# The tokens of the last two expert places, not of the last alone, get ends of their own in a decoder layer with experts

## The chip, the cores and the metric

One core of a Trainium2 chip runs the whole layer as one program. The metric is the device time of one execution in microseconds, the median of several. The kernel before takes 2732.44 us, the median of 3 runs (2731.12 to 2740.7).

## What is computed

One decoder layer over 4096 tokens of width 1024: attention heads and gated recurrent heads side by side, a residual, and then a mixture of experts. Only its last part matters here:

```
h = rmsnorm(x, ln2_pre) * (1 + sc2) + sh2
g_w, g_idx = top_k(softmax(h @ w_rg + b_rg), 1)          # 1 of 4 groups
e_w, e_idx = top_k(softmax(e_logits[of that group]), 2)  # 2 of its 8 experts
ys  = (silu(h @ w_gate[e]) * (h @ w_up[e])) @ w_down[e]  # for both experts
y   = sum over both of ys * weight
out = x + ga2 * rmsnorm(y, ln2_post)
```

Each token meets two experts of one group. Its end, the norm of the sum and the addition to x, needs both results.

## The kernel before, in words

**Sweeps.** `sweep1` and `sweep2` compute the first part. `sweep2` writes x to `out`, the normed tokens to `h_d`, and routes batches of tokens (`g_route`, line 1469): for each of a token's two choices a row of three words (token, row of its result, weight) is scattered to the table `tab_d`, at a slot of its expert, and the token's number to the list `list_d`, in the order of its group. `g_const` (line 1181) fills both tables beforehand. Experts are then ordered by load into 32 places: 8 places for each group, each with a fixed capacity (`CAPS`, line 1717; places 28 to 31 have 256 rows, two tiles of 128).

**Between.** `order` (line 1720) gathers the table by places, transposes its three columns on TensorE, and gets `tokid`, `yrow` and `wgt` for each place, and `last`, tokens and rows of place 31.

**Experts.** `experts` (line 1842) runs the places 0 to 31 on TensorE. For each: load gate, up and down weights (1 MB each, by SP, into the ring `WS` of 4 slots), split each into a high and a low part (ScalarE and VectorE, ring `W` of 8), gather the tokens (GpSimd, ring `XG` of 4), transpose and split them (ring `XT` of 13), gate and up products (`gate_up`), activation, and down products (`down`, line 1924), whose weighted results `g_put` (line 2138) scatters by GpSimd to `y_d`, one row for each choice of each token, the two rows of a token next to each other.

**Ends.** The 4096 tokens of the list are 32 tiles, 8 for each group. `g_fin(m)` (line 2186) ends tile m when all places of its group have put their results: SP reads the tile's 256 rows (1 MB) into a slot of `YY` (2 slots) or, for the last group, of `WS` or `W`; VectorE adds the pairs, ScalarE squares and sums, GpSimd computes the norm's factor (`rstd`, two small operations named `rfv` and `rfr`), VectorE scales, and GpSimd adds the rows to `out` by an indirect store (`put_out`), one small store to `spacer` ahead of it. Entries of the list that lie past the end are skipped by the store.

The tokens of place 31, the last, are not ended through the list. `g_list` (line 2163) writes zeros to their rows of `y_d` and puts a number past the end in their places in the list. `g_other` (line 2213) gathers the results of their other choices from `y_d`, once all other places have put theirs. `down` for place 31 adds this to its product, and `g_last` (line 2155) norms and stores it (`rlv`, `rlr`, `out_dram<-y,last`). `list_rows` (line 1795) computes the indices for this. The last group's list tiles wait for the gathers of `g_other`:

```
rings = [YY]
if g == 3:
    while ("other", tile_n[31] - 1) not in st:
        yield WAIT
    rings += [WS, W]
```

**What sets the order.** All of this is written as generators (lines of work), which `Weave` (line 159) interleaves by a modelled clock: a line goes on when what it names (a tile, an engine) is ready by that clock. So the order on each engine is fixed when the program is built. Each engine's queue is then taken in that order, and a wait stands in front of all that was put behind it: SP's queue carries the weight loads and the reads of `y_d`, GpSimd's all indirect transfers, the small norm operations and the stores to `out`. Transfers that write the same tile, or read what another wrote, wait for the earlier one to land, except where `no_dep` (line 289) says that they don't touch the same rows.

The profile gives line 140 for nearly every instruction, because a wrapper there records them; groups are told apart by tile.

Of the kernel before, what the change touches and what calls it, by code (L numbers as in the profile page):

```python
# [21 lines left out]
P = 128  # L22
# [250 lines left out]
class Layer:  # L273
# [59 lines left out]
    def setup(self, ctx):  # L333
# [807 lines left out]
    def sweep2(self, w16a):  # L1141
# [7 lines left out]
        with ExitStack() as ctx:  # L1149
# [31 lines left out]
            def g_const():  # L1181
# [38 lines left out]
                fill = op.tile([P, D], F32, name="xr")  # L1220
                nc.gpsimd.memset(fill, float(16 * T))
# [247 lines left out]
            def g_route(m):  # L1469
# [85 lines left out]
                nc.vector.tensor_sub(gm[:, 3], gm[:, 3], gm[:, 2])  # L1555
                pl = tile([P, RB, 2, 3], F32, "pl2", 2)[:, :B]
                nc.vector.tensor_copy(pl[:, :, :, 0], bc(idi[:, n0:n0 + B], 2))
# [162 lines left out]
    def order(self, cp, rp, rps):  # L1720

        nc, T, NT = self.nc, self.T, self.NT
        cnt = self.place[:, 1]
# [27 lines left out]
        pt = rps.tile([P, 3, P], F32, name="ps_x")  # L1751
        for o in range(3):
            nc.tensor.transpose(pt[:, o], trow[:, :, o], self.ident)
# [41 lines left out]
    def list_rows(self, cp, rp):  # L1795
# [16 lines left out]
        nc.vector.tensor_scalar(out, out, 1, None, op0=ALU.logical_shift_right)  # L1812
        other = cp.tile([P, 4], I32, name="other")
        nc.vector.tensor_scalar(other, self.yrow[:, P - 4:], 1, None, op0=ALU.bitwise_xor)
        yield
        of = rp.tile([P, 2, 4], F32, name="of4")
        nc.vector.tensor_copy(of[:, 0], out)
        nc.vector.tensor_copy(of[:, 1], other)
        yield
        nc.vector.scalar_tensor_tensor(out, gid[:, 3:4].to_broadcast([P, 4]), float(T), of[:, 0],  # L1820
                                       op0=ALU.mult, op1=ALU.add)
        nc.vector.tensor_scalar_min(other, of[:, 1], float(2 * T - 1))
        self.other = other
# [18 lines left out]
    def experts(self):  # L1842
# [5 lines left out]
        with ExitStack() as ctx:  # L1848
# [74 lines left out]

            def down(avs, wd, j, m, y, wgt, other=None):
                for c in range(2):
                    yield ["ps_d"]
                    pd = ps_d.tile([P, 512], F32, name="ps_d")[:m]
                    for f in range(2):
                        yield [avs[f]]
                        for n, (u, v) in enumerate(((0, 0), (1, 0), (0, 1))):  # L1930
                            nc.tensor.matmul(pd, avs[f][:, u, j * P:j * P + m], wd[f][:, v, c * 512:(c + 1) * 512],
                                             start=(f == 0 and n == 0), stop=(f == 1 and n == 2))
                    v = slice(c * 512, c * 512 + 512)
                    if other is None:
                        self.copy(y[:m, v], pd, wgt)
                    else:
                        nc.vector.scalar_tensor_tensor(y[:m, v], pd, wgt, other[:m, v], op0=ALU.mult, op1=ALU.add)
# [49 lines left out]
            with tc.For_i(0, n_over, 1) as it:  # L1987
# [6 lines left out]
                nc.vector.tensor_scalar_min(oi[:, 1:2], oi[:, 1:2], float(32 * T - 1))  # L1994
                pf = fp.tile([P, 3], F32, name="pf")
                self.gather(pf, self.tab_d, oi[:, 1:2])
# [120 lines left out]
            def g_down(r, avs):  # L2117
# [5 lines left out]
                for j in range(tile_n[r]):  # L2123
                    m = min(P, C - j * P)
                    y = yield from Y.take()
                    wgt = self.wgt[:m, 4 * r + j:4 * r + j + 1]
                    if r < 31:
# [7 lines left out]
                    we.add(g_last(y, o, j, m), first=True)  # L2135
# [18 lines left out]

            def g_last(y, o, j, m):

                yield [y]
                yield from norm(y[:m], o[:m], "rl")
                put_out(y[:m], self.last[:m, 0, j:j + 1])

            ti = cp.tile([P, NT], I32, name="ti")

            def g_list():
# [22 lines left out]
            def g_fin(m):  # L2186
# [96 lines left out]
```

## Time and profile before

| | before |
|---|---|
| median of 3 runs | 2732.44 us |
| profiled execution: own time | 2765.53 us |
| profiled execution: span | 2763.8 us |
| TensorE busy | 2510.2 us (91%) |
| VectorE busy | 1905.7 us (69%) |
| ScalarE busy | 1360.1 us (49%) |
| GpSimd busy | 756.7 us (27%) |
| mean granted TensorE clock | 0.961 of 2.4 GHz |

The span is the time from the first to the last instruction of the profiled execution; its own time is that of the whole execution. Profiling makes it longer than the median of the plain runs. Busy time is the time in which an engine worked on some instruction. Times within the span are counted from its start.

### The profile page before, as it was taken

Reading aid. Unit: us, or ns where it says so; the run is one execution under the profiler, and the core shown is the slowest. Engines: PE = TensorE matmul, PEld = TensorE weight load, DVE = VectorE, ACT = ScalarE, POOL = GpSimd, SP = SyncE. Lnnn points to the kernel's source line nnn. Section 1 sums busy time; section 2 is a strip of 40 time slices with the busy share of each in tenths; the row PEclk is TensorE's granted clock in tenths of the full one; section 3 lists DMA queues with packets and bytes.
Section 4 is the critical chain, followed back from the end, with each engine's and each line's share of the span. In section 5 each row is a group of like instructions: output and inputs, shape, how many; then the busy total and the mean of one; then the engine's idle time right before and its main releaser. Section 6 shows DMA issues by size and latency. Waiting matters only on the chain. (4 is left out here: it accounts for less than half of the span.)

```text
span 2763.8 us, 50275 instructions
## 1 busy us (share of the span) xinstructions
PE 2510.2 (91%) x19433; PEld 1916.5 (69%) x19433; DVE 1905.7 (69%) x4109; ACT 1360.1 (49%) x2935; POOL 756.7 (27%) x1069
## 2 busy tenths in 40 slices
PE   5989999999999999989999999955999999999992
PEld 2767677677667676666666676624888888889981
DVE  5657657777776688878778778664555666566774
ACT  4435444334333355555555545523545656666662
POOL 0111212211211012132232331343442333233336
PEclk9999999999999999999999999977999999999996
DMA  8212222222222334343453453445655878788987
GB/s 278 88 62 77 96 72 73 83 91 75 70 88 83 109 119 126 119 93 97 117 117 93 108 115 94 77 129 187 215 174 188 295 258 270 280 274 286 324 284 215
DMA packets 194619, 414.46 MB, mean 150 GB/s; under 512 B 89069, under 2 KB 124057, under 8 KB 172873
## 3 DMA queue, kind: packets, MB, share of 16 engines
q1 hardware_dynamic: 157216, 319.06, 36.6%
q0 software_dynamic: 31584, 91.58, 11.3%
q8 instruction: 153, 2.51, 0.4%
q10 hardware_dynamic: 5576, 0.58, 0.2%
q14 instruction: 90, 0.73, 0.1%
HBM read 284.60 MB, written 118.16 MB: 146 GB/s over the span
## 5 line engine op out<-in xcount | busy, mean ns | idle before, releaser
L140 PE MATMUL ps_g<-xT,w 128*128 128x256 f32 (+8 forms) x3072 | 461.5, 305 | 0.0
L140 PEld LDWEIGHTS ps_g<-xT,w 128*128 128x128 f32 x3072 | 436.2, 189 | 7.1 <-issue 0.3
L140 PE MATMUL ps_j<-w,mT 128*128 128x512 f16 x1536 | 368.2, 384 | 0.0
L140 PE MATMUL ps_j<-hT,w 128*128 128x256 f16 x3072 | 349.0, 274 | 4.9 <-POOL hT L140 4.9
L140 PE MATMUL ps_j<-w,hT 128*128 128x512 f16 x1536 | 349.7, 380 | 0.0
L140 PEld LDWEIGHTS <-w 128*128 128x128 f16 x3072 | 301.9, 98 | 47.1 <-issue 8.4
L140 PEld LDWEIGHTS <-hT 128*128 128x128 f16 x2304 | 196.6, 99 | 167.2 <-issue 6.7
L140 PE MATMUL ps_d<-w,av 128*128 128x512 f32 (+6 forms) x1020 | 269.1, 407 | 3.9 <-ACT av L140 3.5
L140 ACT ACTIVATE w<-ws 128x512 fp32r<-128x512 f32 (+1 forms) x392 | 246.1, 678 | 32.5 <-issue 23.5
L140 DVE TENSOR_TENSOR w<-ws,w 128x512 fp32r<-128x512 f32 x384 | 245.3, 685 | 5.4 <-ACT w L140 5.3
L140 PEld LDWEIGHTS <-mT 128*128 128x128 f16 x1536 | 144.3, 99 | 148.4 <-issue 12.3
L140 DVE TENSOR_TENSOR xT<-ps_x,xT 128x256 fp32r<-128x256 f32 (+8 forms) x256 | 115.5, 472 | 170.3 <-ACT xT L140 160.2
L140 PE MATMUL ps_j<-hT,w16a 128*128 128x256 f16 x1920 | 222.4, 275 | 0.0
L140 PEld LDWEIGHTS ps_d<-w,av 128*128 128x128 f32 (+6 forms) x1020 | 177.6, 182 | 51.6 <-ACT av L140 5.2
L140 PEld LDWEIGHTS <-w16a 128*128 128x128 f16 x1920 | 188.1, 99 | 25.7 <-issue 0.6
L140 POOL TENSOR_TENSOR hT<-hf,hT 128x512 f16<-128x512 f32 x64 | 103.6, 1619 | 270.0 <-ACT hT L140 255.2
L140 ACT ACTIVATE y<-ps_d,wgt 128x512 f32<-128x512 f32 (+4 forms) x144 | 99.0, 688 | 121.2 <-PE ps_d L140 88.5
L140 PE MATMUL ps_x<-ident,xg 128*128 128x128 f32 (+7 forms) x680 | 127.4, 294 | 28.5 <-DMA xg<-h_d,tok 23.9
L140 ACT ACTIVATE s<-s,mx,qsc 128x256 f32<-128x256 f32 (+1 forms) x256 | 148.8, 584 | 0.0
L140 PEld LDWEIGHTS ps_x<-ident,xg 128*128 128x128 f32 (+7 forms) x680 | 106.3, 193 | 56.5 <-DMA xg<-h_d,tok 28.3
L140 ACT ACTIVATE xT<-ps_x 128x256 fp32r<-128x256 f32 (+8 forms) x256 | 101.3, 422 | 88.5 <-PE ps_x L140 80.2
L140 POOL DMA_INDIRECT y_d<-y,yrow x85 | 91.1, 1072 | 193.3 <-ACT y L140 153.9
(397 smaller groups left out, 4242.3 us busy)
## 6 DMA issues: line engine op xcount, KB each, us to landing
ws<-in_w_exp_gate_dram SPq DMA_DIRECT2D x32, 1024.0 KB
ws<-in_w_exp_up_dram SPq DMA_DIRECT2D x32, 1024.0 KB
ws<-in_w_exp_down_dram SPq DMA_DIRECT2D x32, 1024.0 KB
yy<-y_d SPq DMA_DIRECT2D x24, 1024.0 KB
x<-in_x_dram SPq DMA_DIRECT2D x32, 512.0 KB
hT_d<-hT SPq DMA_DIRECT2D x16, 1024.0 KB
m_w<-in_w_ada_dram SPq DMA_DIRECT2D x128, 128.0 KB
hT<-hT_d SPq DMA_DIRECT2D x16, 1024.0 KB
```

What stands on the lines that cost most here:

```text
L140: r = f(*a, **kw)
```

## The change

Places 30 and 31 both have their ends apart from the list. Place 30's results are stored twice: once as before, as a row for each choice, but to a tensor of its own, `y30_d`, by a plain store of SP; and once added to the other choice's result in a tile `total`, which is normed and stored to `out`. Tokens with choices in both places are ended with place 31: its tile gets its other half from `y_d` first, and then, for those tokens alone, from `y30_d`. For this each row of the table carries a fourth word, the slot of the token's other choice. The last group's list tiles wait for places 24 to 29 alone and for the load of place 31's down weights, and their rings are `YY`, `WS`, and `W` only if place 31's weights are all split by then. The diff, cut to its core:

```diff
-        self.tab_d = d.tile([32 * T, 3], F32, name="tab_d")
+        self.tab_d = d.tile([32 * T, 4], F32, name="tab_d")
+        self.y30_d = d.tile([self.caps[30], D], F32, name="y30_d")
...
-                for c in range(0, 96 * T // P, D):
-                    n = min(96 * T // P - c, D)
-                    nc.sync.dma_start(v[:, c:c + n], fill[:, :n])
+                for c in range(0, 128 * T // P, D):
+                    nc.sync.dma_start(v[:, c:c + D], fill)
...
                 for c in range(2):
                     nc.vector.tensor_tensor(sl[:, c], sf[:, c], gm[:, 4 * c], op=ALU.add)
+                    nc.vector.tensor_tensor(pl[:, :, 1 - c, 3], sf[:, c], gm[:, 4 * c], op=ALU.add)
...
-        trow = rp.tile([P, P, 3], F32, name="trow")
+        trow = rp.tile([P, P, 4], F32, name="trow")
...
-        for o in range(3):
+        for o in range(4):
             nc.tensor.transpose(pt[:, o], trow[:, :, o], self.ident)
...
-        self.last = cp.tile([P, 2, 4], I32, name="last")
-        nc.vector.tensor_copy(self.last, pt[:, 0:2, P - 4:])
+        self.last = cp.tile([P, 2, 8], I32, name="last")
+        nc.vector.tensor_copy(self.last, pt[:, 0:2, P - 8:])
+        self.mate = cp.tile([P, 8], F32, name="mate")
+        nc.vector.tensor_copy(self.mate, pt[:, 3, P - 8:])
...
+        both, in_ = rp.tile([P, 2, 4], F32, name="both"), rp.tile([P, 2, 4], F32, name="in")
+        for i in range(2):
+            nc.vector.scalar_tensor_tensor(both[:, i], self.place[:, 0, 31 - i:32 - i].to_broadcast([P, 4]), -float(T),
+                                           self.mate[:, 4 * i:4 * i + 4], op0=ALU.mult, op1=ALU.add)
...
+        self.near = cp.tile([P, 4], I32, name="near")
+        nc.vector.tensor_scalar_add(self.near, near, float(T))
...
                     if other is None:
                         self.copy(y[:m, v], pd, wgt)
+                        if total is not None:
+                            nc.vector.scalar_tensor_tensor(total[:m, v], pd, wgt, total[:m, v],
+                                                           op0=ALU.mult, op1=ALU.add)
...
-                    while ("other", j) not in st:
+                    while ("other", r, j) not in st:
                         yield WAIT
-                    o = st["other", j]
+                    o = st["other", r, j]
+                    if r == 30:
+                        yield from down(avs, [v[0] for v in wd], j, m, y, wgt, None, o)
+                        we.add(g_put(y, r, j, m))
+                        junk = yield from XT.take()
+                        we.add(g_last(o, junk.rearrange("p u c -> p (u c)").bitcast(BF)[:, :D], r, j, m))
+                        continue
...
             def g_put(y, r, j, m):
                 yield [y]
-                put_y(y, self.yrow[:m, 4 * r + j:4 * r + j + 1], m, "y%d" % (r // 8))
+                g = 4 if r == 30 else r // 8
+                if r == 30:
+                    nc.sync.dma_start(self.y30_d[j * P:j * P + m, :], y[:m])
+                else:
+                    put_y(y, self.yrow[:m, 4 * r + j:4 * r + j + 1], m, "y%d" % g)
                 Y.drop(y)
-                st["left", r // 8] = st.get(("left", r // 8), sum(tile_n[r // 8 * 8:min(r // 8 * 8 + 8, 31)])) - 1
+                n = tile_n[30] if r == 30 else sum(tile_n[8 * g:min(8 * g + 8, 30)])
+                st["left", g] = st.get(("left", g), n) - 1
...
-                for j in range(tile_n[31]):
-                    m = min(P, caps[31] - j * P)
-                    put_y(y, self.yrow[:m, P - 4 + j:P - 3 + j], m, "y3")
-                    self.scatter(self.list_d, self.last[:m, 1, j:j + 1], none[:m], "none", "other rows of the list",
-                                 bounds_check=4 * T - 1, oob_is_err=False)
-                    yield 3000.0
+                for r in (30, 31):
+                    for j in range(tile_n[r]):
+                        m, i = min(P, caps[r] - j * P), 4 * (r - 30) + j
+                        put_y(y, self.yrow[:m, P - 8 + i:P - 7 + i], m, "y3")
+                        self.scatter(self.list_d, self.last[:m, 1, i:i + 1], none[:m], "none%d" % r,
+                                     "other rows of the list", bounds_check=4 * T - 1, oob_is_err=False)
+                        yield 3000.0
...
                 if g == 3:
 
-                    while ("other", tile_n[31] - 1) not in st:
+                    while ("ws", 31, 2) not in st:
                         yield WAIT
-                    rings += [WS, W]
+                    rings += [WS]
+                    if ("w", 31, 2, 1) in st:
+                        rings += [W]
...
                 while st.get(("left", 3), 1):
                     yield WAIT
-                for j in range(tile_n[31]):
-                    m = min(P, caps[31] - j * P)
-                    o = yield from XG.take()
-                    self.gather(o[:m], self.y_d, self.other[:m, j:j + 1])
-                    st["other", j] = o
+                for r in (30, 31):
+                    for j in range(tile_n[r]):
+                        m, i = min(P, caps[r] - j * P), 4 * (r - 30) + j
+                        o = yield from XG.take()
+                        while r == 31 and st.get(("left", 4), 1):
+                            yield WAIT
+                        self.gather(o[:m], self.y_d, self.other[:m, i:i + 1])
+                        if r == 31:
+                            self.gather(o[:m], self.y30_d, self.near[:m, j:j + 1],
+                                        bounds_check=caps[30] - 1, oob_is_err=False)
+                        st["other", r, j] = o
```

`g_last` stores with the index of place 30 or 31 and, for place 30, gives the tile back to `XG`.

## Rows read from the trace of the kernel before

**Rows 1.** The chain that ended last: its shares by line, and its last piece (start us, us, what).

```profile
by line: POOL out_dram L140 0.7%; POOL rfv L140 0.2%; issue 0.2%; POOL rfr L140 0.1%; POOL rlv L140 0.0%; POOL spacer L140 0.0%; POOLq L140 0.0%; POOL rlr L140 0.0%; POOLq L2279 0.0%
...
2749.58 1.56 POOL out_dram L140
```

**Rows 2.** Windows: us; busy PE, PEld, DVE, ACT, POOL (x); clock, DMA share, GB/s.

```profile
2676.00:2700.00 24.00, 23.45 (x173) 21.85 (x172) 17.39 (x30) 15.39 (x31) 6.77 (x10) 1.00 0.69 224
2700.00:2740.00 40.00, 9.60 (x52) 7.28 (x50) 25.58 (x26) 12.24 (x22) 32.08 (x38) 0.70 1.00 310
2740.00:2744.00 4.00, 0.00 (x0) 0.00 (x0) 1.50 (x2) 0.00 (x0) 3.58 (x5) 0.50 0.02 3
...
2714.00:2751.00 37.00, 0.00 (x0) 0.00 (x0) 19.91 (x17) 8.47 (x16) 32.83 (x36) 0.53 0.89 220
```

**Rows 3.** Timeline of PE: start, us, what [idle before]. Places 30 and 31, last products.

```profile
2672.85 9.52 PE L140 MATMUL ps_g<-xT,w 128*128 128x256 f32 x78
...
2691.60 11.68 PE L140 MATMUL ps_g<-xT,w 128*128 128x256 f32 x96
...
2708.36 3.06 PE L140 MATMUL ps_d<-w,av 128*128 128x512 f32 x12 [0.36 <-DVE y L140]
```

**Rows 4.** Timeline of POOL, from place 29's last store into the tail.

```profile
2674.55 1.32 POOL L140 DMA_INDIRECT y_d<-y,yrow  x1 [2.17 <-ACT w L140]
...
2690.03 1.23 POOL L140 DMA_INDIRECT y_d<-y,yrow  x1 [6.14 <-ACT y L140]
...
2692.95 0.99 POOL L140 DMA_INDIRECT y_d<-y,yrow  x1 [1.61 <-ACT y L140]
2698.12 0.99 POOL L140 DMA_INDIRECT xg<-y_d,other  x1 [4.18 <-PE ps_g L140]
2699.41 0.96 POOL L140 DMA_INDIRECT xg<-y_d,other  x1 [0.30 <-issue]
...
2706.44 1.98 POOL L140 DMA_INDIRECT out_dram<-yy,ti  x1 [0.26 <-issue]
...
2710.23 0.19 POOL L140 TENSOR_SCALAR rlv<-srl 128x1 f32<-128x1 f32 x1 [0.90 <-ACT xg L140]
...
2714.57 1.17 POOL L140 TENSOR_SCALAR rlv<-srl 128x1 f32<-128x1 f32 x1 [3.51 <-ACT xg L140]
...
2716.60 2.56 POOL L140 DMA_INDIRECT out_dram<-y,last  x1 [0.20 <-issue]
...
2723.35 0.19 POOL L140 TENSOR_SCALAR rfv<-srf 128x1 f32<-128x1 f32 x1
```

**Rows 5.** SP's queue: a wait (us in total, times, longest), and two issues of its timeline.

```profile
SPq L140 <- DMA out_dram<-yy,ti: 13.3, 1, 13.3
...
2688.78 0.33 SPq L140 DMA_DIRECT2D yy<-y_d  x1
2697.37 1.55 SPq L140 DMA_DIRECT2D ws<-y_d  x3
```

**Rows 6.** Timeline of DVE: last splits of the down weights, places 30 and 31.

```profile
2676.83 1.89 DVE L140 TENSOR_TENSOR w<-ws,w 128x512 fp32r<-128x512 f32 x3
...
2698.80 1.33 DVE L140 TENSOR_TENSOR w<-ws,w 128x512 fp32r<-128x512 f32 x2
```

**Rows 7.** Groups of POOL: tail (2714.5 to 2751.2), then 2400 to 2676. busy us, mean ns | idle before.

```profile
L140 POOL TENSOR_SCALAR rfv<-srf 128x1 f32<-128x1 f32 x7 | 5.7, 815 | 0.6
L140 POOL TENSOR_TENSOR rfr<-rfv,mhalf 128x1 f32<-128x1 f32 x7 | 4.8, 679 | 0.6
...
L140 POOL TENSOR_TENSOR rfr<-rfv,mhalf 128x1 f32<-128x1 f32 x11 | 6.8, 620 | 0.9
L140 POOL TENSOR_SCALAR rfv<-srf 128x1 f32<-128x1 f32 x11 | 2.2, 199 | 33.5 <-ACT yy L140 33.3
```

**Rows 8.** Instructions on tile xg: the product with an add. ns min/median/max.

```profile
L140 DVE SCALAR_TENSOR_TENSOR y<-ps_d,wgt,xg x3: 742/751/752, 2707.6 to 2711.9; 128x512 f32<-128x512 f32 x3
```

**Rows 9.** Timeline of PE between the sweeps and the experts.

```profile
1888.69 0.91 PE L140 MATMUL ps_x<-ident,trow 128*128 128x128 f32 x3 [24.02 <-DMA trow<-tab_d,trows]
```

More of the change, by code (lines that the diff above doesn't have):

```diff
@@ L1220, in g_const @@
                 fill = op.tile([P, D], F32, name="xr")
-                nc.gpsimd.memset(fill, float(16 * T))
+                nc.gpsimd.memset(fill, float(40 * T))
                 v = self.tab_d.rearrange("(p n) o -> p (n o)", p=P)
-                for c in range(0, 96 * T // P, D):
-                    n = min(96 * T // P - c, D)
-                    nc.sync.dma_start(v[:, c:c + n], fill[:, :n])
+                for c in range(0, 128 * T // P, D):
+                    nc.sync.dma_start(v[:, c:c + D], fill)
                 filli = op.tile([P, T // 32], I32, name="xr")
@@ L1555, in g_route @@
                 nc.vector.tensor_sub(gm[:, 3], gm[:, 3], gm[:, 2])
-                pl = tile([P, RB, 2, 3], F32, "pl2", 2)[:, :B]
+                pl = tile([P, RB, 2, 4], F32, "pl2", 2)[:, :B]
                 nc.vector.tensor_copy(pl[:, :, :, 0], bc(idi[:, n0:n0 + B], 2))
@@ L1745, in order @@
         yield
-        trow = rp.tile([P, P, 3], F32, name="trow")
+        trow = rp.tile([P, P, 4], F32, name="trow")
         self.gather(trow.rearrange("p c o -> p (c o)"), self.tab_d.rearrange("(r c) o -> r (c o)", c=P), self.trows)
         yield
-        pt = rps.tile([P, 3, P], F32, name="ps_x")
-        for o in range(3):
+        pt = rps.tile([P, 4, P], F32, name="ps_x")
+        for o in range(4):
             nc.tensor.transpose(pt[:, o], trow[:, :, o], self.ident)
@@ L1812, in list_rows @@
         nc.vector.tensor_scalar(out, out, 1, None, op0=ALU.logical_shift_right)
-        other = cp.tile([P, 4], I32, name="other")
-        nc.vector.tensor_scalar(other, self.yrow[:, P - 4:], 1, None, op0=ALU.bitwise_xor)
+        other = cp.tile([P, 8], I32, name="other")
+        nc.vector.tensor_scalar(other, self.yrow[:, P - 8:], 1, None, op0=ALU.bitwise_xor)
         yield
-        of = rp.tile([P, 2, 4], F32, name="of4")
+        of = rp.tile([P, 3, 8], F32, name="of4")
         nc.vector.tensor_copy(of[:, 0], out)
         nc.vector.tensor_copy(of[:, 1], other)
+        nc.vector.tensor_copy(of[:, 2], self.last[:, 0])
+        both, in_ = rp.tile([P, 2, 4], F32, name="both"), rp.tile([P, 2, 4], F32, name="in")
+        for i in range(2):
+            nc.vector.scalar_tensor_tensor(both[:, i], self.place[:, 0, 31 - i:32 - i].to_broadcast([P, 4]), -float(T),
+                                           self.mate[:, 4 * i:4 * i + 4], op0=ALU.mult, op1=ALU.add)
         yield
-        nc.vector.scalar_tensor_tensor(out, gid[:, 3:4].to_broadcast([P, 4]), float(T), of[:, 0],
+        nc.vector.tensor_scalar(in_, both, 0.0, None, op0=ALU.is_ge)
+        nc.vector.scalar_tensor_tensor(out, gid[:, 3:4].to_broadcast([P, 8]), float(T), of[:, 0],
                                        op0=ALU.mult, op1=ALU.add)
-        nc.vector.tensor_scalar_min(other, of[:, 1], float(2 * T - 1))
+        nc.vector.tensor_scalar_min(of[:, 1], of[:, 1], float(2 * T - 1))
+        near = rp.tile([P, 4], F32, name="near")
+        nc.vector.tensor_scalar_add(near, both[:, 1], float(-T))
+        yield
+        for i in range(2):
+            nc.vector.scalar_tensor_tensor(both[:, i], both[:, i], float(self.caps[31 - i]), in_[:, i],
+                                           op0=ALU.is_lt, op1=ALU.mult)
+        yield
+        nc.vector.scalar_tensor_tensor(self.last[:, 0, 0:4], both[:, 0], float(T), of[:, 2, 0:4],
+                                       op0=ALU.mult, op1=ALU.add)
+        nc.vector.tensor_mul(near, near, both[:, 1])
+        yield
+        nc.vector.tensor_copy(other, of[:, 1])
+        self.near = cp.tile([P, 4], I32, name="near")
+        nc.vector.tensor_scalar_add(self.near, near, float(T))
         self.other = other
@@ L1922, in gate_up, with down @@
                 self.gu = ps
-            def down(avs, wd, j, m, y, wgt, other=None):
+            def down(avs, wd, j, m, y, wgt, other=None, total=None):
                 for c in range(2):
@@ L1935, in down @@
                         self.copy(y[:m, v], pd, wgt)
+                        if total is not None:
+                            nc.vector.scalar_tensor_tensor(total[:m, v], pd, wgt, total[:m, v],
+                                                           op0=ALU.mult, op1=ALU.add)
                     else:
@@ L1994, in experts @@
                 nc.vector.tensor_scalar_min(oi[:, 1:2], oi[:, 1:2], float(32 * T - 1))
-                pf = fp.tile([P, 3], F32, name="pf")
+                pf = fp.tile([P, 4], F32, name="pf")
                 self.gather(pf, self.tab_d, oi[:, 1:2])
@@ L2126, in g_down @@
                     wgt = self.wgt[:m, 4 * r + j:4 * r + j + 1]
-                    if r < 31:
+                    if r < 30:
                         yield from down(avs, [v[0] for v in wd], j, m, y, wgt)
@@ L2130, in g_down @@
                         continue
-                    while ("other", j) not in st:
+                    while ("other", r, j) not in st:
                         yield WAIT
-                    o = st["other", j]
+                    o = st["other", r, j]
[5 more added lines that the diff above has]
+                        continue
                     yield from down(avs, [v[0] for v in wd], j, m, y, wgt, o)
-                    we.add(g_last(y, o, j, m), first=True)
+                    we.add(g_last(y, o, r, j, m), first=True)
                 W.drop(*(v[1] for v in wd))
@@ L2153, in norm, with g_last @@
                 yield
-            def g_last(y, o, j, m):
+            def g_last(y, o, r, j, m):
                 yield [y]
                 yield from norm(y[:m], o[:m], "rl")
+                j += 4 * (r - 30)
                 put_out(y[:m], self.last[:m, 0, j:j + 1])
+                if r == 30:
+                    XG.drop(y)
             ti = cp.tile([P, NT], I32, name="ti")
```

## The prediction

> **What bounds the kernel now.** Lines say nothing here, because one helper (line 140) records every operation, so I read by engine and tile. The chain of waits comes first: over its last piece of time it is GpSimd alone, norms and indirect stores to `out` [rows 1]. The table of windows shows the stage around it [rows 2]: TensorE is full up to 2700 us; from 2714 to 2751 it is idle, and GpSimd is busy for 32.83 of 37 us, the rest being issue gaps. The DMA engines are full from 2700 to 2740 and almost empty for the 4 us after. TensorE's order of work [rows 3] gives the places: 30 has its gate and up products from 2672.85, 31 from 2691.60, and the last down products end at 2711.4. So some 52 us of the 2763.8 us span follow the last product. GpSimd's order of work [rows 4] shows why. The last two stores of place 30's outputs to `y_d` start at 2690.03 and 2692.95. GpSimd then waits 4.18 us for them to land, gathers the other halves of place 31's tokens at 2698.12 and 2699.41, and from there to the end of the last store (2749.58 + 1.56 = 2751.14 [rows 1]) it waits only twice, 0.90 and 3.51 us: 53.0 us, of which 48.6 are work. In these lie the ends of list tiles 22 to 31 and of place 31. The eight reads of the last group (tiles 24 to 31, 1 MB each) are issued from 2697.37, when the stores of place 30 have landed [rows 5].
>
> **The change, part by part.** The sum is made against the profiled execution (span 2763.8 us, own time 2765.53 us). That is 33 us, 1.2%, above the median of 2732.44 us. I take the difference over to the median unscaled.
>
> *The gate.* The last group now waits for places 24 to 29 only. Their last store starts at 2674.55 [rows 4], 18.4 us before that of place 30. This is what can be gained. But the reads also need buffers. A line chooses its rings when it passes the gate; `("w", 31, 2, 1)` is set only after the last split, at 2698.80 + 1.33 us [rows 6], so the `W` ring, which took four of the eight reads before, will not be in the choice. What stays is `YY`, held by tiles 22 and 23, and `WS`, whose slots come free one at a time: that of place 30's down weights at 2678.7 [rows 6], the others with the splits of place 31. And SP takes its queue in order: after 2675 it stands 13.3 us, until 2688.78, in front of tile 23's read, which waits for a store to `out` from its buffer [rows 5]. A read of the last group that was put behind it starts no earlier. So I expect three or four of the eight reads some 5 to 9 us earlier than before, and the rest not earlier. No weight load is behind them, since the gate asks for the last weight load first.
>
> *GpSimd, which sets the end.* Counted from 2698.12:
> - The gathers for place 31 no longer wait for place 30's stores to `y_d`, which are gone (SP stores `y30_d`). They can start at 2693.9, where that store ended: −4.2.
> - The two waits of 0.90 and 3.51 us are filled with list tiles that have landed: −4.4.
> - Place 30 gets two ends of its own. A norm in the tail costs 0.815 + 0.679 us and two gaps of 0.09, 1.67 us [rows 7]; three stores take from 2716.60 to 2723.35 [rows 4], 2.25 each. Two of both: +3.3 and +4.5. The list still has its 32 tiles: rows of place 30 become entries past the end, but the instructions stay, so nothing is saved.
> - Two gathers from `y30_d`, 1.29 us each (2698.12 to 2699.41): +2.6.
> - Each of these writes the tile that the gather before it writes, so GpSimd must wait for that one to land, and all that is queued behind stands too: tiles 22 and 23, place 30's ends, then the last group. No row shows such a pair. Below it could cost 0.3 us, the gap between two gathers that don't depend on each other; above 13.3 us, SP's wait for a store [rows 5]. The nearest row is GpSimd's own wait for the stores to `y_d`, 4.18 us, and I take it for both: +8.4.
> - One norm of place 30 fits into the 6.14 and 1.61 us in which GpSimd waits before 2693: −1.7.
>
> The Trainium skill, "DMA: Bandwidth & Descriptors", section "Anatomy of one DMA — SWDGE (gpsimd) path", puts a transfer issued by GpSimd at about 2.0 us plus its bytes by 436 GB/s, 3.2 us for 512 KB; less the instruction's own 1 us that would be an estimated wait of 2.2 us a pair, and this term +4.4 in place of +8.4. The row of this trace is longer: 5.17 us from the start of the store at 2692.95 to the gather behind it; I keep the row.
>
> *The two gathers of place 30's other halves* come at about 2679, after the wait for place 29's stores, in a stretch where GpSimd is busy for 6.77 of 24 us [rows 2]. They are hidden; if not, 2.6 us.
>
> *VectorE and TensorE in place 30.* Four more products with an add, 0.75 us each [rows 8], read the same PSUM tile as the copy on ScalarE: 3 us on VectorE, which is busy for 17.39 of 24 us, and each of the two PSUM buffers is held longer. TensorE may end 1 to 3 us later. That costs nothing as long as GpSimd is behind: place 31's own end is one entry in GpSimd's queue. Without that cover it is these 3 us.
>
> *Before the experts.* Each row of the table has four words: a fourth transpose (0.91 / 3 = 0.3 us [rows 9]), one more small VectorE operation per choice on the way to the last scatters (0.2), a gather with a third more bytes (0.2): +0.7, between 0 and 1.6. The fourth 512 KB fill, the small operations of the earlier batches and of the list, and two more zero stores and list scatters lie beside a full TensorE: 0. The two sets of list scatters now wait for each other once, and the gathers of the next place's tokens behind them run a place ahead, which covers it.
>
> Sum: −4.2 − 4.4 + 3.3 + 4.5 + 2.6 + 8.4 − 1.7 + 0.7 = +9.2 us, so 2732.4 + 9.2 = **2741.6 us**, 0.34% more. About 0.5%, 13.7 us, is what a measurement of this kernel can tell from no change: I forecast no change that can be told, leaning to slower. With the waits at their bounds (0.6 and 26.6 us in place of 8.4) the sum is +1.4 to +27.4.
>
> **Rivals.**
> - *The DMA engines set the end, not GpSimd.* For it: they are full from 2700 to 2740 [rows 2]. Then the early reads gain what was idle before: 0.31 of 24 us, 7.4 us, and the hole of 3.9 us at 2740, less two gathers of 512 KB at the 310 GB/s of that stretch, 3.4 us: −7.9, 2724.5 us. Against it: in the hole GpSimd is busy for 3.58 of 4 us, so the engines wait for it. Chance 0.20, no change that can be told.
> - *The tail really moves a place forward.* All of GpSimd's idle time from 2676 is filled: 17.2 us to 2700 and 4.4 after; its two stores to `y_d` leave (2.3); the new work (3.3 + 4.5 + 2.6 and two gathers 2.6) is added: −10.9. Norms beside the main stage cost 0.199 + 0.620 us in place of 0.815 + 0.679 [rows 7]; eight of them save 5.4. Together −16.3, 2716 us. It needs the ends of list tiles to pass quickly beside the products. Against it: tile 23's read at 2688.78 leads to its store only at 2706.44 [rows 4], the rings are short, and SP stands. Chance 0.14, faster.
> - *Slower: GpSimd stands at the first gather from `y30_d`.* The store of place 30's outputs goes through SP's queue, behind tile 23's read and then up to four reads of 1 MB that the change puts there. With SP released near 2692 (place 30's two gathers delay the store it waits for by some 3 us) and 3.4 us a read at 310 GB/s, the store lands near 2706 instead of 2699. The first wait is then about 11 us, not 4.2: +6.8, together +16, 2748 us. It decides once that wait passes 4.2 + 4.5 = 8.7 us, where the sum passes 13.7. For it: SP's 13.3 us. Against it: the slots of `WS` come free so late that the stores may be ahead of the reads. Chance 0.26.
> - *Nothing is moved*: all reads still come after place 31's weights are split. Then the new work stays and the gate gains nothing; this is near my forecast and in its share.
>
> **How the numbers follow.** Forecast (GpSimd bound, waits of a few us) 0.40; DMA rival 0.20; moved tail 0.14; standing gather 0.26. So faster 0.14, same 0.60, slower 0.26. The range goes from 2719 to 2757: it takes in the DMA rival and the standing gather with some 9 us of further waits, and leaves out most of the moved tail and the upper bound of the waits, 2 in 10.
>
> **What the profile after would show.** Right: the reads of the last group into `yy` and `ws` only, the first ones shortly after 2689; GpSimd's gathers `xg<-y30_d` with waits of some 4 us before them; two more stores `out_dram<-xg,last`; GpSimd without idle time from about 2706 to its last store near 2759. Wrong: stores of tiles 24 to 27 to `out` before 2705 (the moved tail); GpSimd waiting for DMA between its last stores (the DMA rival); a wait of over 9 us before a `y30_d` gather (the standing one); or a TensorE that ends over 5 us later, which would make place 31 itself the end.

## The result, and the profile after

The changed kernel takes 2763.65 us (median of 4 runs, 2761.33 to 2772.59) where the kernel before, beside it, takes 2733.52: ratio 1.0100, 95% interval 1.0080 to 1.0119. Two repeats gave 1.0085 (1.0061 to 1.0109) and 1.0078 (1.0062 to 1.0095). The forecast was 2741.6 and the range ended at 2757: slower than forecast, and out of the range.

The profiled execution after took 2765.36 us (span 2763.4), near its median; that of before had taken 33 us over its own. Profiling is not what made it longer: later profiled executions of the kernel before took 2754.10, 2757.09 and 2733.85 us at medians of 2754.56, 2756.74 and 2734.81. So the two traces are compared from a common event, place 29's first gate product (before, then after):

```profile
2652.71 9.52 PE L140 MATMUL ps_g<-xT,w 128*128 128x256 f32 x78
2635.78 9.52 PE L140 MATMUL ps_g<-xT,w 128*128 128x256 f32 x78
```

From there:

| us after place 29's first product | before | after | difference |
|---|---|---|---|
| place 31's first gate product | 38.9 | 46.5 | +7.6 |
| end of the last down product | 58.7 | 64.4 | +5.7 |
| end of GpSimd's last store to `out` | 98.4 | 121.9 | +23.5 |
| end of the span | 111.1 | 127.6 | +16.5 |

GpSimd's end moves by more than the span, because the DMA engines have less left when it stops: in the 7.1 us ahead of its end their share is 0.95 before and 0.55 after, and behind it they move 72 GB/s for 12.7 us before (2751.14 to 2763.8) and 60 GB/s for 5.7 us after, some 0.9 and 0.3 MB.

TensorE's order of work after, which answers to [rows 3] (start, us, what, idle time before it and what ended it):

```profile
2655.90 9.52 PE L140 MATMUL ps_g<-xT,w 128*128 128x256 f32 x78
...
2673.07 0.69 PE L140 MATMUL ps_x<-ident,xg 128*128 128x128 f32 x2 [6.14 <-DVE xT L140]
...
2682.27 11.68 PE L140 MATMUL ps_g<-xT,w 128*128 128x256 f32 x96
...
2694.91 5.29 PE L140 MATMUL ps_d<-w,av 128*128 128x512 f32 x21 [0.27 <-ACT av L140]
```

TensorE stands 6.14 us in place 30. It waits for VectorE; VectorE's order shows for what:

```profile
2663.10 0.68 DVE L140 TENSOR_TENSOR w<-ws,w 128x512 fp32r<-128x512 f32 x1
2671.07 1.28 DVE L140 SCALAR_TENSOR_TENSOR yy<-yy,rfr,G 128x1024 f32<-128x1024 f32 x1 [7.28 <-POOL rfr L140]
2672.27 0.41 DVE L140 SCALAR_TENSOR_TENSOR th<-th,ps_g 128x256 f32<-128x256 f32 x1
2672.60 0.75 DVE L140 TENSOR_TENSOR xT<-ps_x,xT 128x256 fp32r<-128x256 f32 x2
```

The norm of a list tile needs `rfr`, 0.57 us of work on GpSimd; VectorE stands 7.28 us for it, and `xT`, for which TensorE waits, is behind. GpSimd's order, which answers to [rows 4], shows what holds it up:

```profile
2657.60 1.31 POOL L140 DMA_INDIRECT y_d<-y,yrow  x1 [1.99 <-ACT w L140]
2667.90 0.97 POOL L140 DMA_INDIRECT xg<-y_d,other  x1 [8.98 <-PE ps_g L140]
2669.18 0.95 POOL L140 DMA_INDIRECT xg<-y_d,other  x1 [0.30 <-issue]
2670.19 0.19 POOL L140 TENSOR_SCALAR rfv<-srf 128x1 f32<-128x1 f32 x1
2670.47 0.57 POOL L140 TENSOR_TENSOR rfr<-rfv,mhalf 128x1 f32<-128x1 f32 x1
...
2674.59 1.51 POOL L140 DMA_INDIRECT xg<-y_d,other  x1 [0.30 <-issue]
2687.40 1.30 POOL L140 DMA_INDIRECT xg<-y_d,near  x1 [11.30 <-DMA y_d<-y]
2689.01 0.96 POOL L140 DMA_INDIRECT xg<-y_d,other  x1 [0.30 <-issue]
2699.06 1.00 POOL L140 DMA_INDIRECT xg<-y_d,near  x1 [9.09 <-DMA xg<-y_d,other]
...
2743.23 0.19 POOL L140 TENSOR_SCALAR rfv<-srf 128x1 f32<-128x1 f32 x1 [6.77 <-ACT ws L140]
...
2756.07 1.61 POOL L140 DMA_INDIRECT out_dram<-yy,ti  x1 [1.56 <-DVE yy L140]
```

The view leaves buffer numbers out, so `y30_d` reads `y_d` here; the gathers from it are those by `near`. Three gathers stand: place 30's first by `other` for 8.98 us, and the two by `near` for 11.30 and 9.09. (The first row names PE's `ps_g`, which had ended at 2666.94; the gather reads what place 29's stores write, and the last part of the second, issued at 2657.60, landed at 2667.14 in the trace, the later of the two.) In between, GpSimd does nothing: the window from 2676 to 2700 has it busy for 3.31 us, against 6.77 [rows 2].

```profile
2676.00:2700.00 24.00, 23.38 (x144) 19.76 (x142) 15.10 (x25) 12.05 (x23) 3.31 (x4) 1.00 0.79 282
2700.00:2740.00 40.00, 0.19 (x1) 0.00 (x0) 19.66 (x17) 6.87 (x12) 32.26 (x43) 0.54 0.68 149
2740.00:2744.00 4.00, 0.00 (x0) 0.00 (x0) 2.42 (x2) 1.15 (x2) 0.69 (x3) 0.50 1.04 363
```

SP's queue, which answers to [rows 5], has the reads of the last group, eight as before (the single `yy` at 2683.91 is tile 23's):

```profile
2667.27 0.33 SPq L140 DMA_DIRECT2D ws<-y_d  x1
2679.94 3.56 SPq L140 DMA_DIRECT2D y_d<-y  x2
2683.91 0.32 SPq L140 DMA_DIRECT2D yy<-y_d  x1
2685.17 47.84 SPq L140 DMA_DIRECT2D ws<-y_d  x5
2733.12 0.94 SPq L140 DMA_DIRECT2D yy<-y_d  x2
```

They use `yy` and `ws` only. The first is 31.5 us after place 29's first product (before 44.7, [rows 5]), the second 49.4, later than the second of before; the last three come only at 2732.7 to 2733.6. The chain of work that ended last runs over them: it leaves GpSimd for 17.9 us, first until a store's data has landed and its buffer is free, then for the read into that buffer.

```profile
2722.68 9.96 DMA out_dram<-ws,ti
2732.70 7.89 DMA ws<-y_d
```

### The profile page after: what moved, and what is told of

It is laid out like the page before. It is cut to its first block, busy times and chain, and to the rows that moved or that the text cites. A ratio compares the mean times of both kernels' runs of the same rounds, so it can differ in the third digit from the quotient of the medians.

```text
span 2763.4 us, 50360 instructions
## 1 busy us (share of the span) xinstructions
PE 2500.3 (90%) x19434; PEld 1913.3 (69%) x19434; DVE 1912.3 (69%) x4145; ACT 1361.2 (49%) x2939; POOL 766.9 (28%) x1085
## 5 line engine op out<-in xcount | busy, mean ns | idle before, releaser
L140 PE MATMUL ps_d<-w,av 128*128 128x512 f32 (+6 forms) x1020 | 262.9, 402 | 2.0 <-ACT av L140 1.7
L140 PEld LDWEIGHTS ps_d<-w,av 128*128 128x128 f32 (+6 forms) x1020 | 176.3, 180 | 49.4 <-ACT av L140 3.5
L140 ACT ACTIVATE y<-ps_d,wgt 128x512 f32<-128x512 f32 (+5 forms) x144 | 99.1, 688 | 114.4 <-PE ps_d L140 82.0
L140 POOL DMA_INDIRECT xg<-h_d,tok x85 | 88.3, 1039 | 202.5 <-PE ps_x L140 181.7
```

The lines of the kernel that those rows point to most:

```text
L140: r = f(*a, **kw)
```

## The experiments

Ratios are to the kernel before, run side by side in the same session (the recorded texts say "call"). That kernel's own median was 2753 and 2755 us in the first and fourth session and 2734 to 2736 in the others, so absolute times are compared within a session alone. "Stage" is from place 29's first product to the end of the span.

| run | session | median, us | ratio (95%) | stage, us | of it behind the last product |
|---|---|---|---|---|---|
| before again | 1 | 2754.56 | 1.0003 (0.9986 to 1.0021) | 111.2 | 53.0 |
| table_only | 1 | 2755.37 | 1.0008 (0.9991 to 1.0025) | 109.8 | 52.3 |
| ends_only | 1 | 2772.08 | 1.0087 (1.0053 to 1.0120) | 125.7 | 61.6 |
| after again | 2 | 2759.80 | 1.0085 (1.0061 to 1.0109) | 126.8 | 62.4 |
| late30 | 2 | 2750.79 | 1.0050 (1.0035 to 1.0065) | 121.2 | 60.1 |
| near_late | 2 | 2752.08 | 1.0055 (1.0038 to 1.0073) | 116.5 | 51.7 |
| ring_w | 2 | 2761.17 | 1.0083 (1.0058 to 1.0107) | 126.1 | 61.7 |
| all2 | 3 | 2746.62 | 1.0044 (1.0027 to 1.0061) | 110.3 | 48.9 |
| all3 | 3 | 2749.58 | 1.0054 (1.0036 to 1.0073) | 115.9 | 48.7 |
| all2_noput | 3 | 2742.09 | 1.0029 (1.0016 to 1.0041) | 109.5 | 46.9 |
| before, third | 4 | 2756.74 | 1.0007 (0.9993 to 1.0021) | 110.1 | 51.9 |
| all2_again | 4 | 2756.09 | 1.0006 (0.9995 to 1.0017) | 111.0 | 49.7 |
| all2_plan | 4 | 2762.62 | 1.0030 (1.0015 to 1.0044) | 110.8 | 49.4 |
| b_late | 4 | 2757.77 | 1.0011 (0.9999 to 1.0022) | 110.2 | 51.0 |
| before, fourth | 5 | 2734.81 | 1.0002 (0.9990 to 1.0014) | 112.2 | 53.0 |
| after, third | 5 | 2756.98 | 1.0078 (1.0062 to 1.0095) | 126.0 | 61.7 |
| all2, third | 5 | 2745.07 | 1.0032 (1.0015 to 1.0049) | 111.5 | 50.2 |
| all2_list | 6 | 2747.97 | 1.0043 (1.0029 to 1.0057) | 113.4 | 49.8 |

Two runs repeat the kernels unchanged, for traces at their usual time:

> The kernel before once more, unchanged, for a profile whose own time is near its median (the one recorded took 2765.5 us where the median is 2732.4). Both theories expect 2733 us plus or minus 5. Theory E (the ends: waiting gathers and short buffers make the change slower) expects the last down product some 50 to 52 us before the end, as in the recorded profile, and the lost 33 us of that profile somewhere before place 30. Theory P (the plan: the added table word alone shifts the modelled clock and so the order of the second sweep) says nothing more about this run.

> The changed kernel once more, on the chip of the three runs beside it. Its ends take 127.6 us from the first product of place 29 to the end of the span, where those of the kernel before take 111.1. Expected: 126 to 128 us again, and 0.7 to 1.1% above the kernel before in the timed runs.

Both as expected in the stage: 111.2 and 126.8 us. The first one's median was not: 2754.56 us, where 2733 plus or minus 5 was expected; the other executions of the kernel before in that session were as long.

**Table or ends?** The planner orders the second sweep by modelled costs, so the fourth word of the table could have shifted that order. table_only adds the word alone to the kernel before; ends_only is the whole change, with the added table operations kept out of the planner's account:

```diff
+ (nc if c < 96 * T // P else self.tc.nc).sync.dma_start(...)
...
+ self.tc.nc.vector.tensor_tensor(pl[:, :, 1 - c, 3], ...)
```

> The kernel before with only the table's fourth word (fill, two VectorE operations per batch, gather, fourth transpose); ends as before. Theory P (plan) expects about 2763 us, theory E (ends) 2734 us: the 0.7 us that the prediction gave this part.

> The changed kernel, but the two added VectorE operations per routing batch and the fourth fill of the table are kept from the modelled clock, so that every engine's order in both sweeps is that of the kernel before; they are still executed. Theory E (ends) expects about 2763 us, as the changed kernel, and its tail of some 63 us behind the last down product. Theory P (plan of the second sweep) expects 2733 us plus or minus 6. Both at half: 2748.

The word costs nothing that can be told, and the ends without the shift cost as much as the whole. The loss is in the ends.

**The first wait moved.** late30 plans the gathers by `other` 9 us later:

```diff
 while st.get(("left", 3), 1): yield WAIT
+yield 9000.0
```

> The changed kernel; the gathers for place 30 are put 9 us later into GpSimd's order, behind the norm of list tile 21, instead of ahead of it. Theory S (GpSimd stands in front of gathers whose data is not there; what is queued behind it, a norm and then VectorE's splits and TensorE, stands too) expects TensorE's wait of 6.1 us in place 30 to go, place 29's first product to the last down product 58.5 us instead of 64.4, and the whole 3 to 6 us less. Theory B (the last list tiles wait for buffers, and that alone sets the end) expects the 6.1 us to go too, but no more than 2 us of the whole.

Timeline of GpSimd:

```profile
2657.45 0.57 POOL L140 TENSOR_TENSOR rfr<-rfv,mhalf 128x1 f32<-128x1 f32 x1
...
2663.20 1.01 POOL L140 DMA_INDIRECT xg<-y_d,other  x1 [0.76 <-PE ps_x L140]
2664.51 0.96 POOL L140 DMA_INDIRECT xg<-y_d,other  x1 [0.30 <-issue]
2665.78 1.08 POOL L140 DMA_INDIRECT xg<-y_d,other  x1 [0.30 <-issue]
2681.61 1.06 POOL L140 DMA_INDIRECT xg<-y_d,near  x1 [14.75 <-DMA y_d<-y]
2682.98 0.95 POOL L140 DMA_INDIRECT xg<-y_d,other  x1 [0.30 <-issue]
2689.55 1.00 POOL L140 DMA_INDIRECT xg<-y_d,near  x1 [5.62 <-DMA xg<-y_d,other]
```

`rfr` now runs ahead of the gather, and TensorE's wait of 6 us in place 30 is gone. Three smaller ones (1.74, 1.29 and 0.27) are in place 31, and the `near` gathers still stand, 20.4 us in all. The last product comes 61.1 us after place 29's first, less than the 64.4 of the changed kernel but more than the 58.5 expected. The planner also moved half of place 30's down products behind place 31's first gate products, so the 5.6 us of the stage (126.8 to 121.2) are those of the move with this shift.

**The second pair moved.** near_late issues the gathers by `other` of both places first and those by `near` behind them, when place 30 is stored:

```diff
+os = []
 self.gather(o[:m], self.y_d, self.other[:m, i:i + 1])
-while r == 31 and st.get(("left", 4), 1): yield WAIT
...
-if r == 31: self.gather(o[:m], self.y30_d, ...)
+if r == 31: os.append((j, m, o))
...
+while st.get(("left", 4), 1): yield WAIT
+yield 8000.0
+for j, m, o in os: self.gather(o[:m], self.y30_d, ...)
```

> The changed kernel; place 31's two gathers from y_d are issued one behind the other, and the two from y30_d 8 us after place 30's results are stored, instead of each pair together. Theory S expects GpSimd's two waits there (11.30 and 9.09 us) to fall to under 6 us together and the end to come 8 to 12 us earlier. Theory B expects the waits to fall but the end to move by 4 us at most, because the last two reads still wait for stores of earlier tiles to land.

GpSimd, then TensorE:

```profile
2662.48 0.97 POOL L140 DMA_INDIRECT xg<-y_d,other  x1 [8.87 <-PE ps_g L140]
...
2685.31 1.57 POOL L140 DMA_INDIRECT xg<-y_d,near  x1 [0.17 <-issue]
2687.19 1.36 POOL L140 DMA_INDIRECT xg<-y_d,near  x1 [0.31 <-issue]
```

```profile
2667.65 0.69 PE L140 MATMUL ps_x<-ident,xg 128*128 128x128 f32 x2 [6.03 <-DVE xT L140]
```

The two waits are gone; in their stead GpSimd stands 7.38 us for place 30's first sum of squares, which ScalarE has not done yet. The part behind the last product is 51.7 us, 10.7 less. The first wait and TensorE's 6.03 us are still there. So each move takes one of the two pieces, and that piece only.

**Buffers?** The rival was that the last reads come late for want of buffers. ring_w chooses the rings again while it waits, and may take `W`:

```diff
-R, yy = yield from take(rings)
...
+now = rings or ([W] if ("w", 31, 2, 1) in st else []) + [YY, WS]
```

> The changed kernel; a list tile of the last group may take a slot of the ring W as soon as place 31's weights are split, also when it passed the gate before (five of the eight reads get one). Theory B expects SP's waits of some 39 us for stores of ws tiles to go, all reads to be issued by 2700 on the profile's clock, GpSimd's idle 6.8 us and the two waits of 1.56 us at the end to go, and the end 9 to 12 us earlier. Theory S expects the reads to be early too, but the end to move by 3 us at most, since GpSimd's order is late by its standing anyway.

SP, then GpSimd:

```profile
2684.19 2.99 SPq L140 DMA_DIRECT2D ws<-y_d  x2
2687.27 3.16 SPq L140 DMA_DIRECT2D w<-y_d  x5
```

```profile
2708.89 1.17 POOL L140 TENSOR_SCALAR rlv<-srl 128x1 f32<-128x1 f32 x1 [5.15 <-ACT xg L140]
...
2750.18 2.55 POOL L140 DMA_INDIRECT out_dram<-w,ti  x1 [0.22 <-issue]
...
2753.03 1.56 POOL L140 DMA_INDIRECT out_dram<-w,ti  x1 [0.26 <-issue]
```

All reads are issued by 2690.4, counted from place 29 some 42 us earlier than the last two of after, and GpSimd's idle time near the end (6.77 us above) is gone; the stage is 126.1, as without the edit. So late buffers alone do not set the end. Nor was that idle time free: beside the changed kernel of the same session, GpSimd's last gather starts 2.4 us later, a wait of 5.15 us for ScalarE's sum of squares of place 31 is new, and its work takes some 2 us longer. Taking out one path to the end left another that is as long.

**Both moves.** all2 is late30 and near_late together; all3 adds ring_w; all2_noput leaves place 30's ends out.

> Both moves at once: place 30's gathers of the other halves 9 us later, and the two gathers of near rows behind them, only when place 30's results are stored and 8 us later. Theory S (GpSimd's queue stood in front of gathers whose data was not there): the two moves took away different waits, one ahead of TensorE's end and one behind it, so they add: from place 29's first product to the last down product 58 to 61 us, behind it 50 to 53, together 109 to 114 (after 126.8, with the near gathers late alone 116.5), ratio 1.001 to 1.004. Nothing is left of the loss but GpSimd's added instructions, which show as 0 to 3 us. The rival (the near gathers' wait only moves to what is behind it, and the 6 us on TensorE come back through another instruction): 116 or more, ratio 1.005 as each alone.

> The two moves of all2, and the reads of the last list tiles may again go to the weight buffers of place 31 when those are free, as in the kernel before. Theory S: once GpSimd does not stand, the buffers may come to set the end; then 2 to 5 us fewer than all2, ratio 0.999 to 1.002. If GpSimd's row of instructions is the bound still (as with ring_w, where the reads came 40 us earlier and the end stayed), all2 and all3 are within 0.1% of each other.

> all2 without the sum of squares, norm and put of place 30's 256 tokens (their rows of the output are left out; everything else is computed). It measures what the two added ends cost on GpSimd when nothing stands. GpSimd's own time for them by the rows of near_late is 2 times 1.4 to 2.0 (rlv, rlr) and 2 times 2.4 to 3.1 (put with its spacer), 7.6 to 10 us. If GpSimd sets the end throughout, it is faster than all2 by 6 to 10 us (0.2 to 0.4%), ratio 0.998 to 1.001; if the reads of the last list tiles, their DVE work or the DMAs set it, by under 3 us.

The stage is 110.3, 111.0 and 111.5 us in three traces of all2, 110.1 to 112.2 in four of the kernel before: the 15 us of the stage are back, shown by moving the gathers that stood. The sum holds too: 126.8 less 5.6 (late30) less 10.3 (near_late) is 110.9. GpSimd, in all2:

```profile
2684.21 0.19 POOL L140 TENSOR_SCALAR rlv<-srl 128x1 f32<-128x1 f32 x1 [9.86 <-ACT xT L140]
...
2739.77 1.56 POOL L140 DMA_INDIRECT out_dram<-ws,ti  x1 [0.26 <-issue]
```

It still has one long wait, for a sum of squares, and its last store ends 104.1 us after place 29's first product, 5.7 us later than before (98.4). The span does not show this, because only 6.2 us follow that store where 12.7 did: the new ends still cost GpSimd time, and a shorter rest of the DMA engines' work makes up for it.

all3 differs from all2 by 0.1%, inside its interval; its stage is 5.6 us longer, with a wait of 4.75 us ahead of the last products. Leaving place 30's norms and stores out takes 4.5 us off the median, less than the 7.6 to 10 of GpSimd's time, with the intervals overlapping, and 0.8 off the stage: GpSimd then waits 14.4 us for ScalarE's sum of squares of a list tile, where it waits 9.86 for place 30's in all2.

**What is left.** all2's ratio of 1.0044 with a level stage asked for a trace of the kernel before beside it (b_third, all2_again), and then for all three kernels side by side (b_fourth, after_third, all2_third):

> The kernel before unchanged, for a trace beside all2's. If the rest of the loss lies ahead of place 29, place 29's first product starts 5 to 12 us earlier after the start than in the changed kernels of this call, and from there to the end it takes 111 us as in the other two traces. If the rest lies in the stage behind, that takes 100 to 106 us here and the start of place 29 agrees within 4 us. Ratio 1.000, within 0.2%.

> all2 unchanged, on the same chip as its two companions. If its 11 us over the kernel before stand, ratio 1.003 to 1.006; if they were the scatter of one call, 0.9995 to 1.0025.

> The kernel before unchanged. From place 29's first product to the end 110 to 111.5 us; place 0's first product to place 29's 742 to 752. Ratio 1.000, within 0.2%.

> The changed kernel unchanged. Theory S alone (the whole loss stands behind place 29's first product): from there to the end 125 to 128 us, ratio 1.005 to 1.0065 (15 to 17 us). If some 8 us more lie ahead of it, ratio 1.008 to 1.010, and place 29 starts 5 to 12 us later than in the kernel before of this call.

> The repaired kernel unchanged. Theory S alone: from place 29's first product to the end 110 to 111.5 us, ratio 0.9995 to 1.002. If some 8 us lie ahead of place 29: ratio 1.003 to 1.005.

The ratio of all2 is 1.0006 in the fourth session and 1.0032 in the fifth, the stage level in both. TensorE's first product of place 29 in the kernel before, the changed one and all2, fifth session:

```profile
2619.88 9.52 PE L140 MATMUL ps_g<-xT,w 128*128 128x256 f32 x78
```

```profile
2628.87 9.52 PE L140 MATMUL ps_g<-xT,w 128*128 128x256 f32 x78
```

```profile
2635.54 9.52 PE L140 MATMUL ps_g<-xT,w 128*128 128x256 f32 x78
```

So of the 22.8 us between the spans of before (2732.1) and after (2754.9), 13.8 arise behind that point and 9.0 ahead of it; all2 (2747.0) has 15.7 ahead. These are single profiles: in the fourth session the kernel before reached that product later than all2 (2645.18 and 2641.36), and places 0 to 28 alone scatter from 741 to 752 us in the four traces of the kernel before, of which the fifth session's is the shortest. What does repeat in every trace with the new ends: place 2 takes 38 to 41 us (before 33 to 35), places 3 to 7 take 133 to 137 (141 to 149) and places 8 to 16 take 236 to 244 (230 to 233). TensorE's waits for tokens move with them: in the fifth session it stands 5.8 us in places 3 to 7 before and not at all after, in places 8 to 16 3.7 before and 6.9 after. In place 2 the gathers of the list's rows stand 5.05 us behind four scatters to the list, and the gathers of place 3's tokens behind them (changed kernel, fifth session):

```profile
1938.45 0.98 POOL L140 DMA_INDIRECT ti<-list_d,lrow  x1 [5.05 <-DMA list_d<-none,last]
```

all2_list moves the list's gathers behind the tokens':

```diff
 Y.drop(y)
+yield 6000.0
 for m in range(NT):
     self.gather(ti[:, m:m + 1], self.list_d, ...)
```

> all2, and the gathers of the list's rows planned 6 us later, so that the three gathers of place 3's tokens stand ahead of the first of them on GpSimd and not behind its 5 us of waiting. Theory S in its third place: place 2 takes 34 to 36 us (all2: 39.2 to 39.8; the kernel before 32.8 to 35.0), TensorE's wait for those tokens 3 to 5 us in place of 9; ratio 0.999 to 1.0025 (all2 had 1.0006, 1.0032 and 1.0044). The rival (places 3 to 7, which are 5 to 8 us shorter with the change, give the gain back, because the order there only shifts): place 2 as forecast, ratio within 0.1% of all2, 1.002 to 1.0045.

Place 2 still takes 39.8 us, which neither theory had; the ratio is the rival's. The first gather of the tokens and the matmul that waits for it, in the changed kernel (fifth session) and in all2_list:

```profile
1939.74 0.96 POOL L140 DMA_INDIRECT xg<-h_d,tok  x1 [0.30 <-issue]
```

```profile
1943.94 0.48 PE L140 MATMUL ps_x<-ident,xg 128*128 128x128 f32 x1 [6.73 <-DMA xg<-h_d,tok]
```

```profile
1938.44 0.97 POOL L140 DMA_INDIRECT xg<-h_d,tok  x1 [0.30 <-issue]
```

```profile
1949.77 0.48 PE L140 MATMUL ps_x<-ident,xg 128*128 128x128 f32 x1 [7.80 <-DMA xg<-h_d,tok]
```

Counted from place 0's first product (1880.0 and 1884.9) the gather is 6.2 us earlier, and its matmul 0.9 later: the transfer takes 11.3 us in place of 4.2. So the place in GpSimd's queue alone does not set the time here; the transfer takes longer. In both kernels SP issues two weight loads of 1 MB 52.5 to 55.5 us after place 0's first product. The gather of all2_list, at 53.5, falls among them, that of the changed kernel, at 59.7, behind them, which fits; and two more zero stores of 512 KB stand ahead. Neither was tried. Nor is the plan's shift the cause: all2_plan is all2 with the table operations kept out of the account, by the edit of ends_only.

> all2, with the two added operations of each routing batch and the fourth fill DMA kept out of the planner's account, so that the order of both sweeps is the kernel before's. Theory P2 (the shifted order costs 5 to 10 us ahead of place 29, which the stage behind cannot show): ratio 0.999 to 1.001, place 29's first product 5 us or more earlier than in all2. Theory E (the order is worth nothing, as table_only and ends_only said): within 0.15% of all2, 1.003 to 1.006.

It has no smaller ratio than all2_again beside it. The 0 to 12 us ahead of place 29 stay open.

**Does the kernel before gain from the same idea?** b_late plans the kernel before's two gathers by `other` 5 us later; ahead of them GpSimd stood 4.18 us [rows 4].

> The kernel before, with the two gathers of the other halves of place 31's tokens planned 5 us later. There the first of them waited 4.18 us in GpSimd's queue with rfv and rfr of a list tile behind it. Theory S: the wait goes, 2 to 4 us less behind the last down product, ratio 0.998 to 0.9995. The rival (in the kernel before GpSimd has time again before its row of norms and puts begins, so the wait costs nothing): within 0.1% of the kernel before.

The wait goes (they start at 2685.01 and 2686.34 after 0.19 and 0.30 us), the time doesn't: the rival was right. No version here beats the kernel before.

## Why the prediction was wrong

Of the +9.2 us all but 0.7 were to come behind place 29. There the span lost 13.8 to 16.5 us, and GpSimd's end, by which I counted, 23.5; the rest of the loss lies ahead of place 29 and is open. Two of the signs of being wrong showed: a wait of over 9 us before a gather from `y30_d`, and a TensorE that ended over 5 us later.

**The bound: right in the main.** GpSimd's norms and stores stand last, and moving the gathers that hold them up moves the end. The DMA rival falls with a share of 0.68 from 2700 to 2740 where before had 1.00 [rows 2]. But I took the end of GpSimd's last store over to the span one for one, and 7 us of its 23.5 were taken up behind it. And in the changed kernel the chain that ended last also runs over late buffers; ring_w shows that taking those out alone gains nothing.

**The two waits: mechanism right, the term mis-sized.** I took 4.18 us each, 8.4; they measured 11.30 and 9.09, 20.4, within the bound of 26.6 (18.5 and 17.9 in the two repeats). near_late puts 10.3 us of stage on them. The standing-gather rival had the first wait at about 11 us, but for the wrong reason: SP's store of place 30 was behind one read only. GpSimd reached the gather at 2676.1, while place 30's down products ran until 2682.4; its two stores were issued at 2679.94 and 2683.18 and still had to land. I had put the gathers where [rows 4] has them, behind place 30, and the change's order puts them ahead. The second wait is for the gather by `other` that was issued at 2689.01: 10.05 us until the next could start, and 7.8 in the fifth session. By the Trainium skill's "DMA: Bandwidth & Descriptors", section "Anatomy of one DMA — SWDGE (gpsimd) path", it would be an estimated 3.2 us. The trace does not agree; the DMA engines' share was 0.91 from 2689 to 2699, and the measurement decides.

**"The two gathers of place 30's other halves are hidden": wrong, the step that failed outright.** I put them at nothing, since GpSimd had little busy time there, and did not ask what is queued behind a gather whose data has not landed. The first waited 8.98 us, and with it `rfr`, VectorE (7.28) and TensorE (6.14): late30 takes 5.6 us off the stage.

**"TensorE later costs nothing as long as GpSimd is behind": half right.** It ended 5.7 us later, by this chain and not by the four added products (0.75 us each, as forecast). Place 31's ends are in GpSimd's queue, so late30 shortened the end too.

**The gate: half right, and worth nothing.** The rings were `YY` and `WS`, as forecast. But one read came earlier, by 13 us, where I had three or four by 5 to 9, and the others came later than before. The waits of 0.90 and 3.51 us are gone (−4.4 forecast), and 6.77 and twice 1.56 us stand instead.

**Before the experts: no cost that can be told**, as forecast (table_only). But "the gathers run a place ahead, which covers it" was wrong for place 2, which is some 5 us longer; what that is worth after places 3 to 16 stays open.

**Added ends:** +3.3 and +4.5 were GpSimd's time. all2_noput finds 0.8 us of stage for both, and 4.5 of the median that cannot be told from none: GpSimd waits longer for ScalarE once this work is gone.

## What to carry to other kernels

An indirect gather waits in its engine's queue for the data that it reads, and everything behind it waits too: price the place in the queue against the landing of its data, not the engine's busy share, and follow the small operations behind it (here 0.57 us of GpSimd) to the engines that need them. When such a wait is found, move the gather behind the work that is ready; three waits so moved gave the 15 us of this stage back. Not every such wait costs time: the same move gained nothing in the kernel before (b_late), and neither did an earlier place for a gather whose data then took longer to come (all2_list). A resource that is idle in the profile is not free if its queue is ordered.

## What had not been expected of the hardware

After the 6 us in which TensorE stood, it did not come back at full speed at once. In the changed kernel of the fifth session the wait ends at 2666.14. The granted clock from 2666 to 2667 is 0.50 of 2.4 GHz, the lower level of 1.2, and from 2667 to 2676 it is 0.89. Nine gate products right behind the wait took 2.27 us, where nine ahead of it had taken 1.31:

```profile
2658.77 1.31 PE L140 MATMUL ps_g<-xT,w 128*128 128x256 f32 x9
...
2666.49 2.27 PE L140 MATMUL ps_g<-xT,w 128*128 128x256 f32 x9
```

And a gather of 512 KB that was issued 6.2 us earlier landed no earlier, as in all2_list.
